# A hybrid decoder layer on one Trainium2 core: nine places for the early adaLN weights, and every second weight piece of the middle split by way of PSUM

## The chip, the cores and the metric

One core of one Trainium2 chip runs the whole program. The metric is the device time of one execution in microseconds (us). The engines are PE (TensorE matmul) and its weight loads PEld, DVE (VectorE), ACT (ScalarE), POOL (GpSimd) and SP (SyncE); each takes its instructions in program order, and SP and ACT also issue transfers.

## What is computed

One decoder layer in fp32 for 512 prompt tokens and 8 sample tokens, held as 520 columns. The part that matters here:

```python
sh1, sc1, g1, sh2, sc2, g2 = adaln(c, w_ada, b_ada)       # silu(c) @ w_ada + b_ada, in six parts
h = rmsnorm(x, pre1_g) * (1 + sc1) + sh1
... = jnp.split(h @ w_in, SPLIT_OFFSETS, axis=-1)         # then DeltaNet heads and sparse attention
mix = jnp.concatenate([o_a, o_b], axis=-1) @ w_out
x = x + g1 * rmsnorm(mix, post1_g)
h = rmsnorm(x, pre2_g) * (1 + sc2) + sh2
f = jnp.square(jax.nn.relu(h @ w_ff1)) @ w_ff2
x = x + g2 * rmsnorm(f, post2_g)
```

## The kernel before

**Three products for one.** Each fp32 product is made of three PE passes in a rounded format. A weight tile `wr` and an activation are each split into a high part (`wh`, `hh`) and the rest (`wl`, `hl`): ACT rounds (`wh = copy(wr)`, L327 or L431) and DVE subtracts (`wl = wr - wh`, L328). `mm3` then issues `wh*hh`, `wh*hl` and `wl*hh` (L446 to L448).

**The list of operations.** `run` writes one list of operations with the weights that each needs. `sub` hands out the next split piece; it also issues loads some items ahead (`load_to`) and splits some pieces ahead into a ring of six 512-column slots. Raw `wr` tiles have four places. A tile scheduler then sets each engine's order by what it expects to be ready. All loads of weights are issued by SP, in program order: a load that waits for a place holds every load behind it.

**The head.** The layer's inputs `x` (16 transfers), the constants and then the adaLN weights for the first norm (`wd`, 64 items of 512 KB, kind "ada") come in. `wd` tiles have four places (`L`, tag "d", `ND` = 4), and `LOOK` = 5 items are loaded ahead. The 16 blocks of the model dimension are taken in five parts, `PARTS`, of 2, 2, 4, 4 and 4 blocks. For each part `ada_part` multiplies the `wd` items (L590), sums the four column groups with a small matmul (L600), and `modulate` makes `hh` and `hl` of the part. Between two parts, `early` multiplies the finished part with eight weight columns while the `wd` of the next part go by. `norm` makes the row scale R of the first rmsnorm: a sum over partitions on PE (L310), a reciprocal root on DVE (L294 to L300), a transpose on PE (L275). It stands behind seven of the first part's eight `wd` items (`NORM` = 7).

**The middle.** `wout` multiplies with w_out (16 tiles). `mid` then makes the second norm's input for each half of the columns: `residual` (L1844 to L1861) scales `y`, adds x, squares and sums on DVE, ACT and POOL together; a second rmsnorm follows (L1890 to L1901), and the result is split into `h2h` and `h2l`. While it runs, PE is in `wout` or `ff1` on the other half. `xsums` then adds and splits the operands `T` of the later stage. Weights are split by `split1` here: ACT, then DVE with both inputs in SBUF.

**The units.** The later matmuls (`ff1_unit`, `ff2_unit`) use seven products for eight. Their weights go through `split_staged`: ACT rounds, ACT also copies `wr` into PSUM (`stg`, L436), and DVE subtracts with one input from PSUM (L437). POOL makes sums of weights (L374) meanwhile.

Of the kernel before, what the change touches and what calls it, by code (L numbers as in the profile page):

```python
# [9 lines left out]
F32 = mybir.dt.float32  # L10
# [35 lines left out]
NE = 8  # L46
PARTS = ((0, 2), (2, 4), (4, 8), (8, 12), (12, 16))
ADA0 = [[4 * k0 + 2 * (k1 - k0) * v for v in range(2)] for k0, k1 in PARTS]
NORM = 7
LOOK = 5  # L50
AD0 = 8
RY = 2
MY = 1
# [184 lines left out]
class Kern:  # L238
# [4 lines left out]

    def __init__(self, ctx, tc, I, O):
        self.ctx, self.tc, self.nc, self.I, self.O = ctx, tc, tc.nc, I, O
        self.jobs, self.more = [], None

    def open(self, name, side="left", **kw):
        st = ExitStack()
# [102 lines left out]
    def load_to(self, k):  # L352
        while self.iload <= min(k, len(self.items) - 1):
            ap, kind = self.items[self.iload]
            if kind == "more" and not self.more:
                return
            if kind == "ada":
                t = self.L("wd", [128, 1024])
            elif kind == "more":
                t = self.more()  # L360
            else:
                t = self.wp.tile([128, 1024], F32, name="wr", bufs=4)[:, :ap.shape[1]]
            self.nc.sync.dma_start(t, ap)
            self.raw[self.iload] = t
            self.iload += 1
# [10 lines left out]
    def sub(self):  # L376
# [4 lines left out]
            for key in [key for key in d if (key[0] if d is self.sums else key) < k]:  # L381
                del d[key]
        look = 7 if isinstance(now, str) else 4 if self.items[min(k + 4, len(self.items) - 1)][1] == "more" else 2
        self.load_to(k + (LOOK if self.items[min(k + LOOK, len(self.items) - 1)][1] == "ada" else look))
        while self.sumq and self.sumq[0][0] <= i + 2 + SL:
            _, ku, name = self.sumq.pop(0)
            self.wsum(ku, name)
        while self.icut < len(self.subs) and (self.icut <= i + 2 or self.ahead < 3):
# [7 lines left out]
            if not src:  # L396
                self.load_to(k)
                self.cut[self.icut] = self.raw[k]
            else:
                if src is True or src[0] == "A":  # L400
                    k += 0 if src is True else UNIT.index(src)
                    self.load_to(k)
                    wr = self.raw[k][:, o:o + n]
                else:
                    wr = self.sums[k, src][:, o:o + n]
                self.held[self.icut] = self.need(n)
                if n > 512 and self.slot % 2:
                    self.slot = (self.slot + 1) % RING
                a = 512 * self.slot
                self.slot = (self.slot + (n + 511) // 512) % RING  # L410
                wh, wl = self.wh[:, a:a + n], self.wl[:, a:a + n]
                if n > 512 and self.stage:
                    self.split_staged(wr, wh, wl)
                else:
                    self.split1(wr, wh, wl)
                self.cut[self.icut] = (wh, wl)
                self.ahead += 1
# [10 lines left out]
    def split_staged(self, x, hh, hl):  # L428

        nc = self.nc  # L430
        nc.scalar.copy(hh, x)  # L431
        n = x.shape[1]
        for o in range(0, n, self.stage[1]):
            s = slice(o, o + self.stage[1])
            p = self.stage[0].tile([128, self.stage[1]], F32, name="stg")
            nc.scalar.copy(p, x[:, s])  # L436
            nc.vector.tensor_tensor(hl[:, s], p, hh[:, s].bitcast(F32), op=OP.subtract)  # L437

# [92 lines left out]
    def head(self):  # L531
# [2 lines left out]
        hp, self.close_hp = self.open("hp", "right")  # L534
        self.hh = hp.tile([128, KT, NT], F32R, name="hh")
        self.hl = hp.tile([128, KT, NT], F32R, name="hl")
        self.kp, self.close_kp = self.open("kp")
        self.U, self.close_U = self.open("U")
        self.ada_tile = lambda: self.B("ada_t", [128, 16, 32])
        self.vacc = {}  # L540
        cr = self.B("cr", [128, 16, 9])
# [5 lines left out]
        nc.vector.tensor_scalar(cr, cr, 0.5, None, op0=OP.mult)  # L547
        nc.vector.scalar_tensor_tensor(self.cs[:, :, 0:9], th, 1.0, cr, op0=OP.add, op1=OP.mult)
        self.x = [self.B("x", [128, NT]) for _ in range(KT)]
        for kt in range(KT):  # L550
            nc.sync.dma_start(self.x[kt], I["x"][:, kt])
        nc.sync.dma_start(self.cst, I["cst"])
        self.xs = self.S("xs", [128, KT, NS])
        nc.scalar.dma_start(self.xs, I["xs"])
        ss = self.B("ss", [128, NT])
# [1 line left out]
        for kt in range(1, KT):  # L557
            sq = self.B("sq", [128, NT])
            nc.scalar.activation(sq, self.x[kt], AF.Square)
            nc.vector.tensor_tensor(ss, ss, sq, op=OP.add)  # L560
        self.mod[0], self.mod[1] = (self.kp.tile([128, 16, 9], F32, name=f"ada{v}") for v in range(2))
        self.aq, self.ssx = {}, ss

    def norm(self):
# [1148 lines left out]
            self.gate(h, accs, getattr(self, "mx", None))  # L1713

    def open_in(self):
        self.ptab = self.kp.tile([1, 256], I32, name="ptab")
        self.nc.scalar.dma_start(self.ptab, self.I["pt"])
        self.kn = self.S("kn", [128, 2])
# [5 lines left out]
    def open_mix(self):  # L1724
# [2 lines left out]
        self.flush()  # L1727
        nc.scalar.dma_start(self.O["convp"], self.cpo)
        nc.scalar.dma_start(self.O["convs"], self.stc)
        self.close_U()  # L1730
        self.close_kp()
        mx, self.close_mx = self.open("mx")
        self.mx = (mx.tile([128, KT, NT], F32R, name="mh"), mx.tile([128, KT, NT], F32R, name="ml"))
        self.U, self.close_U = self.open("U2")
# [22 lines left out]
    def open_out(self):  # L1757
# [6 lines left out]
        self.h2 = {0: self.parts(self.V1, "a", "h2")}  # L1764
        self.y = [[self.V1.tile([128, 4, HF], F32, name="y", tag="a") for _ in range(4)] for _ in range(2)]
        self.more = lambda: self.V1.tile([128, 1024], F32, name="wd2", tag="s")
        self.wo, self.close_wo = self.open("wo", "right")
        self.ada_tile = lambda: self.V1.tile([128, 16, 32], F32, name="ada_t", tag="s")
        self.gate_gain(2, 1, self.wo)
# [359 lines left out]
    def open_accs(self, shape, wide, bufs):  # L2129

        p, c1 = self.open("psu", space=PSUM)
        q, c2 = self.open("pst", bufs=bufs, space=PSUM)
        self.stage = q, wide
        self.acc = lambda n: p.tile(shape, F32, name=f"acc{n}")
        self.close_accs = lambda: (c2(), c1())

# [144 lines left out]
```

## Time and profile before

| | |
|---|---|
| median of three runs | 2828.99 us (2827.51 to 2833.29) |
| the profiled execution | 2828.82 us |
| its span, first to last instruction | 2827.1 us |
| PE busy | 2681.5 us, 95% of the span |
| DVE, ACT, POOL busy | 60%, 56%, 40% |
| mean granted TensorE clock | 0.979 of full speed |

The profile lists the busy time of each engine, groups of instructions by line, what each wait ended with, and any stretch of time by itself. PE's records have modelled ends, so a busy PE may still be slow: the count of its matmuls in a stretch tells more. [...] "Idle before <- X" names the instruction or transfer whose end came last.

### The profile page before, as it was taken

The page shows a single profiled execution, that of the slowest core. Times are in us where ns is not written, and L with a number is a line of the kernel's source. Part 1 is how long each engine was busy: PE and PEld are TensorE (multiplying, and loading weights), DVE is VectorE, ACT ScalarE, POOL GpSimd, SP SyncE. Part 2 cuts the span into 40 slices and gives each one's busy share as a digit, 9 for nine tenths or more (in the row PEclk, how much of TensorE's full clock was granted, in tenths as well). Part 3 has the DMA queues.
Part 4 walks back from the last instruction along what each step waited for, and adds up shares of the span by engine and source line. Part 5 has one row for each costly group of instructions (what it writes and reads, how often), then busy time and mean ns, then how long its engine had stood idle before and what let it go on. Part 6 is the DMA issues. An engine that isn't in the chain of part 4 may idle for free.

```text
span 2827.1 us, 56292 instructions
## 1 busy us (share of the span) xinstructions
PE 2681.5 (95%) x21584; PEld 2484.1 (88%) x21584; DVE 1693.7 (60%) x3338; ACT 1573.3 (56%) x2780; POOL 1127.3 (40%) x907
## 2 busy tenths in 40 slices
PE   6999999999999999999998999999998999999996
PEld 3589977788888877888887999999998999999996
DVE  4465493357585455642687555555556677776767
ACT  3134322234544443233566677777778888887763
POOL 0000011123103342221454665656567777777514
PEclk9999999999999999999998999999999999999998
DMA  7853466764444555577665434343433333342454
GB/s 262 288 172 74 122 193 209 217 193 140 158 155 155 167 157 178 184 244 254 232 220 158 157 117 146 117 146 118 145 132 128 133 137 129 142 144 102 138 173 157
DMA packets 195126, 466.15 MB, mean 165 GB/s; under 512 B 25609, under 2 KB 76170, under 8 KB 194858
## 3 DMA queue, kind: packets, MB, share of 16 engines
q1 hardware_dynamic: 165616, 421.83, 44.8%
q10 hardware_dynamic: 27194, 36.53, 4.3%
q0 software_dynamic: 2048, 4.21, 0.5%
q8 instruction: 170, 2.79, 0.4%
q14 instruction: 98, 0.80, 0.1%
HBM read 413.57 MB, written 48.91 MB: 164 GB/s over the span
## 4 chain that ended last, share of the span: by engine, by line
PE 64%; DVE 6%; DMA 3%; issue 2%; ACT 2%; POOL 1%; SPq 0%; another core or an unknown queue 0%; ACTq 0%; DVEq 0%; POOLq 0%
PE acc L446 19%; PE acc L448 19%; PE acc L447 19%; DMA wr<-in_win 2%; PE m L481 2%; DVE wl L328 1%; PE m L275 1%; PE m L1140 1%; ACT wh L327 1%; PE m L1117 1%; ACT y L1901 0%; DVE cu L1301 0%; DMA rx<-mixd 0%; PE m L1482 0%; PE m L1639 0%
## 5 line engine op out<-in xcount | busy, mean ns | idle before, releaser
L437 DVE TENSOR_TENSOR wl<-stg,wh 128x512 fp32r<-128x512 f32 (+1 forms) x584 | 490.0, 867 | 308.6 <-ACT wh L431 300.0
L446 PE MATMUL acc<-hh,wh 128*128 128x260 f32 (+1 forms) x1984 | 587.5, 298 | 14.3 <-ACT hh L622 5.7
L447 PE MATMUL acc<-hl,wh 128*128 128x260 f32 (+1 forms) x1984 | 568.1, 287 | 0.4 <-DVE hl L623 0.4
L448 PE MATMUL acc<-hh,wl 128*128 128x260 f32 (+1 forms) x1984 | 566.0, 287 | 1.6 <-DVE wl L328 1.6
L327 ACT CAST wh<-wr 128x512 fp32r<-128x512 f32 (+1 forms) x478 | 284.3, 611 | 462.9 <-DMA wr<-in_win 210.7
L328 DVE TENSOR_TENSOR wl<-wr,wh 128x512 fp32r<-128x512 f32 (+1 forms) x478 | 353.0, 753 | 312.8 <-ACT wh L327 309.1
L448 PE MATMUL acc<-xf,wl 128*128 128x260 f32 x1824 | 516.4, 283 | 4.6 <-DVE wl L328 4.6
L446 PE MATMUL acc<-xf,wh 128*128 128x260 f32 x1824 | 516.7, 283 | 2.5 <-ACT f L2162 1.1
L447 PE MATMUL acc<-xf,wh 128*128 128x260 f32 x1824 | 515.9, 283 | 0.0
L446 PEld LDWEIGHTS acc<-hh,wh 128*128 128x128 f32 (+1 forms) x1984 | 376.3, 190 | 88.6 <-issue 44.7
L447 PEld LDWEIGHTS acc<-hl,wh 128*128 128x128 f32 (+1 forms) x1984 | 377.3, 190 | 7.9 <-DVE hl L623 3.7
L448 PEld LDWEIGHTS acc<-hh,wl 128*128 128x128 f32 (+1 forms) x1984 | 376.4, 190 | 6.6 <-DVE wl L328 4.1
L448 PEld LDWEIGHTS acc<-xf,wl 128*128 128x128 f32 x1824 | 344.3, 189 | 5.0 <-DVE wl L328 4.9
L446 PEld LDWEIGHTS acc<-xf,wh 128*128 128x128 f32 x1824 | 344.3, 189 | 3.1 <-ACT f L2162 1.3
L447 PEld LDWEIGHTS acc<-xf,wh 128*128 128x128 f32 x1824 | 344.0, 189 | 0.0
L436 ACT COPY stg<-S 128x512 f32<-128x512 f32 (+1 forms) x334 | 240.7, 731 | 88.0 <-DVE wl L437 80.3
L448 PE MATMUL acc<-h2h,wl 128*128 128x260 f32 x928 | 267.6, 289 | 10.2 <-DVE wl L328 9.2
L446 PE MATMUL acc<-h2h,wh 128*128 128x260 f32 x928 | 267.2, 288 | 8.0 <-ACT wh L327 4.3
L447 PE MATMUL acc<-h2l,wh 128*128 128x260 f32 x928 | 267.7, 289 | 4.8 <-DVE h2l L328 4.8
L446 PE MATMUL acc<-T,wh 128*128 128x260 f32 x896 | 254.5, 284 | 4.7 <-DVE fr L2008 3.8
L448 PE MATMUL acc<-T,wl 128*128 128x260 f32 x896 | 254.4, 284 | 0.0
L447 PE MATMUL acc<-T,wh 128*128 128x260 f32 x896 | 254.0, 283 | 0.0
(543 smaller groups left out, 5798.6 us busy)
## 6 DMA issues: line engine op xcount, KB each, us to landing
wr<-in_wff SPq DMA_DIRECT2D x256, 512.0 KB
wd<-in_wada SPq DMA_DIRECT2D x106, 512.0 KB
wr<-in_win SPq DMA_DIRECT2D x106, 512.0 KB
wr<-in_wada SPq DMA_DIRECT2D x86, 512.0 KB
wr<-in_wout SPq DMA_DIRECT2D x48, 512.0 KB
st<-f SPq DMA_DIRECT2D x32, 520.0 KB
pg<-in_ckt SPq DMA_DIRECT2D x256, 64.0 KB
wr<-in_wff2l SPq DMA_DIRECT2D x32, 512.0 KB
```

The source lines that it names most:

```text
L275: self.nc.tensor.transpose(out, in_, self.ident[:n, :n])
L327: pin(self.nc.scalar.copy(hh, x))
L328: pin((eng or self.nc.vector).tensor_tensor(hl, x, hh.bitcast(F32), op=OP.subtract))
L436: nc.scalar.copy(p, x[:, s])
L437: nc.vector.tensor_tensor(hl[:, s], p, hh[:, s].bitcast(F32), op=OP.subtract)
L446: T.matmul(acc, wh[:, cs], xh, start=first, stop=False, skip_group_check=goes_on)
L447: T.matmul(acc, wh[:, cs], xl, start=False, stop=False, skip_group_check=goes_on)
L448: T.matmul(acc, wl[:, cs], xh, start=False, stop=last, skip_group_check=goes_on)
L481: self.nc.tensor.matmul(self.aacc[v][32 * g:32 * g + 32, :], self.cs[:, kt, :], w[:, j * 512:(j + 1) * 512], start=(kt == 0), stop=(kt == ...
L1117: nc.tensor.matmul(ps[:, :w], qs[h2][:, 128 * i:128 * (i + 1)], kb[:, :w], start=True, stop=True)
L1140: nc.tensor.matmul(po[:, 0:256], vt[:, kb_ + k], pts[:, 256 * k:256 * k + 256], start=(kb_ + k == 0), stop=(kb_ + k == i))
```

## The change

It changes the head and the middle.

- **Places.** A pool `eb` with five more `wd` places is open during the head; items whose number modulo 9 is under 5 go there, the rest to the four old places. While it is open, 12 items are loaded ahead in place of 5 (`EARLY_LOOK`). It closes in `open_in`, where the pool `kp` now opens, and two small tiles of `kp` move to another pool.
- **Order.** `NORM` goes from 7 to 2, and the load of the constants and of the first `wd` item is written ahead of `x`.
- **Split by way of PSUM.** In the middle (`wout` and the first 16 `ff1` operations) `stage` now stands for the PSUM tiles that small results use, and of the 512-column pieces every second one takes `split_staged`.

```diff
-NORM = 7
+NORM = 2
 LOOK = 5
+FIRST = 1
+EARLY_LOOK = 12
+EB = 5
...
-            if kind == "ada":
+            if kind == "ada" and self.eb and self.iload % 9 < EB:
+                t = self.eb.tile([128, 1024], F32, name="wd", bufs=EB)
+            elif kind == "ada":
                 t = self.L("wd", [128, 1024])
...
-        self.load_to(k + (LOOK if self.items[min(k + LOOK, len(self.items) - 1)][1] == "ada" else look))
+        look = EARLY_LOOK if self.eb else LOOK if self.items[min(k + LOOK, len(self.items) - 1)][1] == "ada" else look
+        self.load_to(k + look)
...
-                if n > 512 and self.stage:
+                if self.stage and (n > 512 or self.icut % 2):
                     self.split_staged(wr, wh, wl)
...
-            s = slice(o, o + self.stage[1])
-            p = self.stage[0].tile([128, self.stage[1]], F32, name="stg")
+            s = slice(o, min(n, o + self.stage[1]))
+            p = self.stage[0].tile([128, self.stage[1]], F32, name="stg", **self.stage[2])
...
-        self.kp, self.close_kp = self.open("kp")
         self.U, self.close_U = self.open("U")
+        self.eb, self.close_eb = self.open("eb")
...
+        nc.sync.dma_start(self.cst, I["cst"])
+        self.load_to(FIRST - 1)
         for kt in range(KT):
             nc.sync.dma_start(self.x[kt], I["x"][:, kt])
-        nc.sync.dma_start(self.cst, I["cst"])
+        self.mod[0], self.mod[1] = (hp.tile([128, 16, 9], F32, name=f"ada{v}") for v in range(2))
...
     def open_in(self):
+        self.close_eb()
+        self.eb = None
+        self.kp, self.close_kp = self.open("kp")
...
         self.more = lambda: self.V1.tile([128, 1024], F32, name="wd2", tag="s")
+        self.stage = self.psm, 512, {"tag": "m"}
```

The lines of the changed file stand 3 to 11 further on: L590 is L597 there, L275 L278, L310 L313, L600 L607, L363 L368, L328 L331, L437 L443, L1844 L1855, L1847 L1858, L1798 L1809.

On SP, the loads behind `x` in the head, before (`wd` and `wr` as above; PE_ and DVE_ are waits for a place or a result of that engine, DMAHW_ a wait for an earlier transfer):

```order
L363 DMA wd<-in_wada 128x1024 [waits DMAHW6_49]
L363 DMA wd<-in_wada 128x1024 [waits DMAHW7_49,PE_49]
L363 DMA wd<-in_wada 128x1024 [waits DMAHW4_49,DMAHW0_49,PE_49]
L363 DMA wd<-in_wada 128x1024 [waits DMAHW5_49,DMAHW1_49,PE_49]
L363 DMA wd<-in_wada 128x1024 [waits DMAHW6_49,DMAHW2_49,PE_49]
L363 DMA wr<-in_win 128x256 [waits DMAHW3_49]
```

The same loads after:

```order
L368 DMA wd<-in_wada 128x1024 [waits DMAHW2_49]
L368 DMA wd<-in_wada 128x1024 [waits DMAHW3_49]
L368 DMA wd<-in_wada 128x1024 [waits DMAHW4_49]
L368 DMA wd<-in_wada 128x1024 [waits DMAHW5_49]
L368 DMA wd<-in_wada 128x1024 [waits DMAHW6_49]
L368 DMA wr<-in_win 128x256 [waits DMAHW7_49]
```

The order is the same; the waits for PE are gone from the fifth to the eighth item. The first loads on SP (c, the constants, the first `wd`, then `x`) stand in the same order in both.

On PE, the start of the program before (four rows of L590 are one `wd` item of the first part; L310 and L275 are `norm`, `ss` its sum of squares, `rq_i` the reciprocal root, `aqs` the summed adaLN product):

```order
L590 MATMUL m<-wd,cs 32x256 x24
L310 MATMUL m<-ones,ss 128x1 x2
L310 MATMUL m<-ones,ss 4x1
L310 MATMUL m<-ones,ss 128x1 x2
L310 MATMUL m<-ones,ss 4x1
L590 MATMUL m<-wd,cs 32x256 x5
L275 MATMUL m<-cst,rq_i 128x128 x2
L275 MATMUL m<-cst,rq_i 128x4
L275 MATMUL m<-cst,rq_i 128x128 x2
L275 MATMUL m<-cst,rq_i 128x4
L590 MATMUL m<-wd,cs 32x256 x3
L600 MATMUL m<-cst,aqs 128x9 x4
```

The same after:

```order
L597 MATMUL m<-wd,cs 32x256 x16
L313 MATMUL m<-ones,ss 128x1 x2
L313 MATMUL m<-ones,ss 4x1
L313 MATMUL m<-ones,ss 128x1 x2
L313 MATMUL m<-ones,ss 4x1
L278 MATMUL m<-cst,rq_i 128x128 x2
L278 MATMUL m<-cst,rq_i 128x4
L278 MATMUL m<-cst,rq_i 128x128 x2
L278 MATMUL m<-cst,rq_i 128x4
L597 MATMUL m<-wd,cs 32x256 x16
L607 MATMUL m<-cst,aqs 128x9 x4
L597 MATMUL m<-wd,cs 32x256 x8
```

`norm` moved ahead of the last four items of the first part, and two items of the next part, not one, now stand ahead of the first `early`.

On DVE, the start of `residual` for the first half in the middle, before (`y` are its steps, `wl` the weight splits):

```order
L328 TENSOR_TENSOR wl<-wr,wh 128x512 x3
L1844 TENSOR_TENSOR y<-y,R 128x1040
L328 TENSOR_TENSOR wl<-wr,wh 128x512
L1798 TENSOR_TENSOR y<-acc,rg 128x8
L1847 TENSOR_TENSOR y<-y,rx 128x1040 x2
L1844 TENSOR_TENSOR y<-y,R 128x1040
L328 TENSOR_TENSOR wl<-wr,wh 128x512 x2
```

The same after:

```order
L331 TENSOR_TENSOR wl<-wr,wh 128x512
L1855 TENSOR_TENSOR y<-y,R 128x1040
L443 TENSOR_TENSOR wl<-stg,wh 128x512
L1809 TENSOR_TENSOR y<-acc,rg 128x8
L1858 TENSOR_TENSOR y<-y,rx 128x1040
L443 TENSOR_TENSOR wl<-stg,wh 128x512
L331 TENSOR_TENSOR wl<-wr,wh 128x512
L1858 TENSOR_TENSOR y<-y,rx 128x1040
L1855 TENSOR_TENSOR y<-y,R 128x1040
L443 TENSOR_TENSOR wl<-stg,wh 128x512
```

Among the steps of `residual`, pieces from PSUM (`stg`) now alternate with pieces from SBUF. Over the program 80 pieces of 512 columns, and the first two pieces of the units (as four of 512), change from SBUF to PSUM: 84 more subtractions with `stg` on DVE and 84 more `stg` copies on ACT. Between the head and the middle, and from the units on, the order of PE, DVE and ACT is the same.

## Rows read from the trace of the kernel before

**Rows 1.** Page, part 1: busy us, share of the span, instructions of each engine.
```profile
PE 2681.5 (95%) x21584; PEld 2484.1 (88%) x21584; DVE 1693.7 (60%) x3338; ACT 1573.3 (56%) x2780; POOL 1127.3 (40%) x907
```
**Rows 2.** Stretches: length; busy us and (instructions) by engine; clock; DMA share, GB/s.
```profile
63.00:92.00 29.00, 26.29 (x158) 16.05 (x160) 12.19 (x29) 3.91 (x9) 0.00 (x0) 0.94 0.80 277
99.00:132.00 33.00, 32.44 (x241) 25.32 (x238) 13.51 (x28) 5.27 (x9) 0.00 (x0) 0.97 0.76 264
...
1385.00:1425.00 40.00, 35.91 (x280) 34.79 (x279) 38.49 (x51) 20.66 (x38) 27.89 (x19) 0.96 0.62 215
1425.00:1445.00 20.00, 16.29 (x112) 15.19 (x111) 17.17 (x28) 17.67 (x33) 7.76 (x4) 0.83 0.37 129
1445.00:1480.00 35.00, 32.24 (x253) 31.62 (x252) 30.50 (x28) 18.07 (x34) 26.18 (x13) 0.95 0.76 242
1480.00:1520.00 40.00, 27.49 (x162) 24.93 (x162) 36.38 (x34) 25.89 (x47) 29.92 (x16) 0.75 0.28 91
1380.00:1580.00 200.00, 173.91 (x1289) 167.96 (x1288) 162.49 (x197) 121.69 (x212) 113.79 (x61) 0.90 0.56 183
1600.00:1800.00 200.00, 200.00 (x1669) 200.00 (x1669) 108.57 (x129) 150.69 (x180) 120.42 (x80) 1.00 0.39 130
```
**Rows 3.** Short stretches of the head, same columns.
```profile
20.00:22.00 2.00, 0.00 (x0) 0.00 (x0) 1.79 (x3) 1.66 (x3) 0.00 (x0) 1.00 1.03 416
...
48.00:52.00 4.00, 4.00 (x39) 2.97 (x38) 0.85 (x2) 1.86 (x6) 0.00 (x0) 1.00 0.53 160
...
68.00:72.00 4.00, 4.00 (x26) 2.43 (x24) 1.43 (x4) 0.41 (x1) 0.00 (x0) 1.00 0.19 21
```
**Rows 4.** Waits of SP's queue, 26 to 175 us: total us, times, longest.
```profile
SPq L363 <- PE m L590: 88.1, 38, 6.9
```
**Rows 5.** Waits of PE, 42 to 175 us, same columns.
```profile
PE m L590 <- DMA wd<-in_wada: 1.6, 2, 1.4
```
**Rows 6.** Timeline of the head on PE: start us, us, what, idle before.
```profile
28.44 2.18 PE L310 MATMUL m<-ones,ss 128*128 128x1 f32 x11
...
32.94 1.69 PE L275 MATMUL m<-cst,rq_i 128*128 128x128 f32 x6 [0.26 <-DVE rms_st L312]
...
34.56 1.07 PE L590 MATMUL m<-wd,cs 128*32 128x256 f32 x6
35.57 1.88 PE L600 MATMUL m<-cst,aqs 128*128 128x9 f32 x8
...
40.08 1.02 PE L446 MATMUL acc<-hh,wh 128*128 128x260 f32 x3 [1.62 <-ACT hh L622]
```
**Rows 7.** A transfer issued by ACT, timeline near the head's end.
```profile
168.31 0.34 ACTq L1721 DMA_DIRECT2D oh<-in_oh  x1
```
**Rows 8.** Weight subtractions by shape in 1220:1380, 1370:1580, 2150:2650: busy us, mean ns.
```profile
L328 DVE TENSOR_TENSOR wl<-wr,wh 128x512 fp32r<-128x512 f32 x66 | 45.7, 693 | 111.7 <-ACT wh L327 111.7
...
L328 DVE TENSOR_TENSOR wl<-wr,wh 128x512 fp32r<-128x512 f32 x96 | 93.1, 1001 | 18.9 <-ACT wh L327 18.9
...
L437 DVE TENSOR_TENSOR wl<-stg,wh 128x512 fp32r<-128x512 f32 x348 | 224.2, 686 | 95.1 <-ACT wh L431 90.3 <-ACT stg L436 4.7
```
**Rows 9.** Timelines of DVE and of POOL in the middle.
```profile
1391.79 2.92 DVE L328 TENSOR_TENSOR wl<-wr,wh 128x512 fp32r<-128x512 f32 x1
1428.43 2.93 DVE L328 TENSOR_TENSOR wl<-wr,wh 128x512 fp32r<-128x512 f32 x1
1436.85 0.16 DVE L314 TENSOR_SCALAR rms_st<-m 128x2 f32<-128x2 f32 x1 [2.45 <-PE m L310]
...
1388.10 6.06 POOL L1844 TENSOR_TENSOR y<-y,R 128x1040 f32<-128x1040 f32 x2 [3.27 <-ACT R L324]
1424.46 6.34 POOL L1890 TENSOR_TENSOR y<-y,R 128x1040 f32<-128x1040 f32 x2 [3.86 <-ACT R L324]
```
**Rows 10.** Waits of PE, 1180 to 1600 us.
```profile
PE acc L448 <- DVE wl L328: 13.0, 8, 3.2
```
**Rows 11.** The copy to PSUM, by shape, 2150:2650: busy us, mean ns.
```profile
L436 ACT COPY stg<-wr 128x512 f32<-128x512 f32 x149 | 87.4, 589 | 37.6 <-DVE wl L437 37.2
```

More of the change, by code (lines that the diff above doesn't have):

```diff
@@ L245, in __init__ @@
         self.ctx, self.tc, self.nc, self.I, self.O = ctx, tc, tc.nc, I, O
-        self.jobs, self.more = [], None
+        self.jobs, self.more, self.eb = [], None, None
     def open(self, name, side="left", **kw):
@@ L560, in head @@
             nc.vector.tensor_tensor(ss, ss, sq, op=OP.add)
-        self.mod[0], self.mod[1] = (self.kp.tile([128, 16, 9], F32, name=f"ada{v}") for v in range(2))
         self.aq, self.ssx = {}, ss
@@ L1729, in open_mix @@
         nc.scalar.dma_start(self.O["convs"], self.stc)
+        self.close_kp()
         self.close_U()
-        self.close_kp()
         mx, self.close_mx = self.open("mx")
@@ L2132, in open_accs @@
         q, c2 = self.open("pst", bufs=bufs, space=PSUM)
-        self.stage = q, wide
+        self.stage = q, wide, {}
         self.acc = lambda n: p.tile(shape, F32, name=f"acc{n}")
```

## Prediction

> **What bounds the kernel now.** I began with the busy times of the page. PE is busy for 2681.5 us of 2827.1 and no other engine comes near it [rows 1], so a gain has to come from time in which PE waits or runs slowly. The second view is the table of stretches, and what to see in it is the number of matmuls. In 1600 to 1800 us, with nothing in PE's way, 1669 matmuls pass in 200 us, one every 0.120 us. From 1380 to 1580 there are 1289, which at that pace is 154.5 us of work: 45.5 us are lost, though PE reads as busy for 173.9 [rows 2]. Of them 6.5 are lost in 1385 to 1425, 6.6 in 1425 to 1445, 4.7 in 1445 to 1480 and 20.6 in 1480 to 1520, by the same count [rows 2]. That is the middle, the one great loss that the diff touches. In the head PE is idle for 2.7 us in 63 to 92 and 0.6 us in 99 to 132, and it had a mean clock of 0.94 in the one and 0.97 in the other [rows 2].
>
> The third view is the waits. In the head SP's queue waits 88.1 us, in 38 waits, for PE to give back a `wd` place [rows 4]. Meanwhile the DMA engines, which moved 416 GB/s while nothing stopped them, fall to 160 and to 21 GB/s [rows 3]. So loads stop and later arrive late, though PE's own named waits for `wd` are only 1.6 us [rows 5]. In the middle PE's named wait is for `wl`, 13.0 us in 8 waits [rows 10], so DVE is what comes last there.
>
> The fourth view tells why DVE is late. A subtraction of 512 columns takes 693 ns in 1220 to 1380, and 1001 ns on average in 1370 to 1580 [rows 8]. The long ones take 2.92 and 2.93 us, and at those moments POOL is in a large operation of `residual` or of the second norm [rows 9]. The same subtraction with one input from PSUM takes 686 ns on average over 348 pieces of the units [rows 8], where POOL is busy 120 of 200 us [rows 2]. I read this as a stall that two SBUF inputs meet beside POOL, and that a PSUM input escapes.
>
> **The change part by part. Places and look-ahead.** Five more places let SP issue the fifth to the eighth item and those behind them without waiting for PE, so the 88.1 us of SP's waits shrink. No time is won by that itself: it is won where data came late. The bounds are 1.6 us, the waits named for `wd` [rows 5], and all the idle time of the two stretches, 3.3 us; I take 2.7, since the rest of the idle time waits for `wr` or a split behind the same blocked queue. To that comes the clock. A mean of 0.94 over 29 us, between the levels 1 and 0.5, is 3.5 us at 1.2 GHz, of which half, 1.7 us, is lost; 0.97 over 33 us loses 1.0. Both stretches are ones in which PE stood idle as well, so half of this 2.7 us should go with the idle time: I take 1.4, with bounds of 0 and 2.7.
>
> **Norm.** `norm` moves from behind six `wd` items, as PE has them, to behind four. Its sum on PE starts at 28.44 and its last transposes end at 34.56 [rows 6]. Two items at 416 GB/s are 2 x 1.26 us [rows 3], so those now end near 32.0. Four items then follow at 1.01 us each (34.56 to 35.57 is one), and the sum over groups (L600), at 35.57 before, comes at 36.1: 0.5 us late. Against it, one more item stands ahead of the first `early`, in PE's wait of 1.62 us for `hh` [rows 6], and that is 1.0 us won. Net -0.5 us; the bounds are +0.5 (the moved item gains nothing) and -1.0. The cover of this edit is that wait for `hh`; without it the 0.5 us are lost. The first loads stand in the same order on SP as before, so writing the constants first costs and gains nothing.
>
> **Pool kp.** It opens at the head's end, so ACT issues three more small loads there. One such issue took 0.34 us [rows 7], together 1.0 us; they stand in front of ACT's splits of the next weights, which are some pieces ahead, so I take 0.4 and keep 0 and 1.0.
>
> The head: -2.7 - 1.4 - 0.5 + 0.4 = -4.2 us, taken as -4. Its ends are -6.5 (3.3 + 2.7 + 1.0 - 0.5) and +1.5 (nothing gained, 0.5 and 1.0 paid).
>
> **Split by way of PSUM.** In 1370 to 1580 there are 96 subtractions of 512 columns, each 308 ns longer than undisturbed: 29.6 us [rows 8]. With every second one at 686 ns, half of it, 14.8 us, is taken off DVE. In the worst stretch DVE is busy 36.4 of 40 us while PE loses 20.6 [rows 2], so most of this reaches PE: I take 12. The order adds something. In the second norm DVE waits 2.45 us for PE's sum [rows 9]; subtractions of `h2l` now stand ahead of that row and fill the wait: I take 2. Fewer gaps also bring back some clock: 1480 to 1520 ran at 0.75 [rows 2], which is half of 40 us at 1.2 GHz and so 10 us lost; I take 2 of them. Against this, PE meets the second norm's sum earlier in its own work: +1, an estimate from the same 2.45 us.
>
> The new work is 84 copies into PSUM of 589 ns [rows 11], 49.5 us of ACT, which is busy 121.7 of 200 us in 1380 to 1580 [rows 2]. What hides it is the 78 us in which ACT has nothing; behind a copy in ACT's queue stand the next `wh` and the steps of `residual`. I put it at nothing, and the second rival has its price. PSUM places of small results are shared with the copies; DVE empties each in 0.69 us.
>
> The middle: -12 - 2 - 2 + 1 = -15 us. Its ends: -25, all 14.8 and the 10 us of clock; and -4, where another chain than DVE's binds (below).
>
> [...]
>
> **Sum.** 2828.8 - 4 - 15 = 2809.8 us, against the profiled execution's 2828.8 (its span and 1.7 us around it). The median is 2829.0, so nothing is to be converted.
>
> **The rivals. First, another chain binds the middle.** PE there waits for `h2h` of the other half in the end, and this comes by the reciprocal root, POOL's steps of 6.06 and 6.34 us for two [rows 9], and ACT. If that chain sets the end, freed DVE time only shortens DVE's own steps in it. I put that at 4 us: the 2.45 us wait and two stalls of the 2.2 us that 2.92 has over 0.69 [rows 9], 6.9 us, of which about half is in the chain. With the head's -4 the time is 2828.8 - 8 = 2821. For it: the 20.6 us are lost in the 40 us just behind the second norm. Against it: DVE is 36.4 of 40 us busy then, and PE names `wl` [rows 10].
>
> **Second, slower: ACT becomes the bound.** A piece of 512 columns feeds 12 matmuls. In 1425 to 1520 there are 112 + 253 + 162 = 527 matmuls, 44 pieces, 22 of them staged: 13.0 us more on ACT. If each copy holds back the next `wh` and nothing there is won, the time is 13.0, less 2.5 gained in 1385 to 1425 and 5 in the head: 2834, and up to 2841 with the head at +1.5. It decides if ACT is full wherever PE waits. For it: 1425 to 1445 holds 9.3 pieces, so 4.7 copies or 2.7 us, and ACT, busy 17.67 of 20, has 2.3 left [rows 2]. Against it: over all 95 us it is busy 61.6 (17.67 + 18.07 + 25.89) and has 33 left for 13 [rows 2].
>
> **Third, the head gives nothing.** The four `wr` places still hold SP's queue, and loads wait behind them as they did behind `wd`. Then the time is 2828.8 - 15 = 2814. For it: PE's named waits for `wd` are only 1.6 us [rows 5]. Against it: SP names PE's L590, not a `wr` place, in 88.1 us [rows 4].
>
> **How the numbers follow.** A measurement of this kernel can tell about 0.2%, 5.7 us, from no change, so faster means under 2823.3. The forecast of 2810 has 0.60, the first rival 0.18, the third 0.11, the second 0.06, and 0.05 is left for no change, where what DVE gains ACT takes. The forecast's own ends are 2828.8 - 6.5 - 25 = 2797 and, with both parts at their poor ends, 2828.8 + 1.5 - 4 = 2826; this takes in the first and third rival, and with the second outside it the range is 2797 to 2826. Faster is 0.84: the forecast, the third rival and most of the first, less 0.05 for poor ends. Same is 0.10 and slower 0.06.
>
> **What the profile after would show.** The head: SP's waits for the `wd` matmuls fall well under 88 us, idle time in 63 to 132 under 1 us. If these waits move to `wr` and PE's idle time stays, the third rival holds. The middle: `wl` from PSUM takes about 0.69 us beside POOL; the mean of all subtractions in 1370 to 1580 falls from 1001 to about 850 ns; 1380 to 1580 holds some 120 more matmuls. If the subtractions shorten and the matmuls do not rise, the first rival holds; if PE then waits for `wh` or `stg` and ACT has no idle time in 1425 to 1520, the second. The forecast is wrong if pieces from PSUM too take over 2 us beside POOL, since then nothing is freed and 49.5 us of ACT are paid.

## The result and the profile after

The changed kernel takes 2805.71 us (median of four runs, 2801.07 to 2812.09) where the kernel before takes 2830.08 (2827.51 to 2833.29). The ratio on record, from all runs, is 0.9931, with a 95% interval of 0.991 to 0.9952: 19.5 us faster, between 14 and 25. The two medians lie 24.4 us apart, inside that interval. The forecast was 19 us, so the total came out right. Its two parts did not: the head won about 11 us in place of 4, the middle some 7 in place of 15.

The first view is the table of stretches, for the whole head and for 260 us of the middle, beginning at the same matmul of the program in both kernels. The columns are those of [rows 2]. The kernel before:

```profile
0.00:230.00 230.00, 197.51 (x1392) 146.32 (x1393) 119.53 (x316) 76.84 (x185) 7.60 (x25) 0.98 0.66 225
1380.00:1640.00 260.00, 233.91 (x1789) 227.96 (x1788) 195.43 (x236) 166.30 (x265) 150.02 (x85) 0.92 0.53 174
```

The changed kernel:

```profile
0.00:230.00 230.00, 200.34 (x1489) 155.79 (x1490) 125.56 (x327) 80.79 (x195) 8.67 (x25) 0.97 0.66 230
1359.80:1619.80 260.00, 234.63 (x1849) 230.22 (x1848) 183.34 (x243) 194.46 (x322) 149.27 (x88) 0.95 0.54 180
```

Read the matmul counts, not PE's busy time. In the first 230 us 97 more matmuls pass, and at 0.120 us each ([rows 2], 1600 to 1800 us) that is 11.6 us. In the middle 60 more pass, 7.2 us, though PE's busy time grew by 0.7 us only. DVE's busy time there fell by 12.1 us, and ACT's rose by 28.2.

The two profiled executions differ by 27.8 us, 9 more than these two parts. The rest lies between the head and the middle, where the order of instructions is the same. From the 1380th matmul of the program to the 10220th the kernel before took 1150.1 us and the changed one 1141.8; over all traces of this study that stretch took between 1141.8 and 1158.3 us with the same instructions. No cause is read from it, and single executions of whole programs are not compared below.

The waits of SP's queue from 20 to 175 us, in the changed kernel:

```profile
SPq L368 <- PE m L597: 59.9, 22, 9.0
SPq L368 <- DVE wl L331: 33.7, 16, 8.8
```

Before, in the same 20 to 175 us, the waits for PE's `wd` matmuls were 90.0 us, and those for a `wr` place that DVE has to give back were these:

```profile
SPq L363 <- DVE wl L328: 7.4, 8, 3.7
```

So the waits for PE fell to 59.9 us, not to near nothing, and waits for `wr` took their place, as the third rival had it: together they are 97.4 us before and 93.6 after. The two stretches of the head that the prediction priced [rows 2], in the changed kernel:

```profile
63.00:92.00 29.00, 26.38 (x157) 15.37 (x157) 14.67 (x32) 7.48 (x14) 0.82 (x2) 0.88 0.91 329
99.00:132.00 33.00, 31.63 (x222) 22.95 (x221) 16.31 (x32) 7.93 (x14) 0.82 (x2) 0.90 0.92 330
```

The loads flow more freely, 329 and 330 GB/s where it was 277 and 264. But PE is idle for 2.6 and 1.4 us, together 4.0 where it was 3.3, and the clock is lower, 0.88 and 0.90 where it was 0.94 and 0.97. The prediction's sign for the head, under 1 us of idle time from 63 to 132, did not come. Both signs of the third rival came, but not its result: the head won 11 us all the same.

DVE's operations by shape from 1350 to 1560 us, busy us and mean ns, in the changed kernel:

```profile
L331 DVE TENSOR_TENSOR wl<-wr,wh 128x512 fp32r<-128x512 f32 x49 | 46.2, 943 | 12.2 <-ACT wh L330 9.3 <-PE acc L454 2.8
L443 DVE TENSOR_TENSOR wl<-stg,wh 128x512 fp32r<-128x512 f32 x52 | 35.2, 684 | 18.8 <-ACT stg L442 13.7 <-ACT wh L437 4.7
L1858 DVE TENSOR_TENSOR y<-y,rx 128x1040 f32<-128x1040 f32 x8 | 16.6, 2072 | 0.0
L331 DVE TENSOR_TENSOR T<-y,T 128x1040 fp32r<-128x1040 f32 x8 | 13.8, 1719 | 1.3 <-ACT T L330 1.3
L331 DVE TENSOR_TENSOR h2l<-y,h2h 128x1040 fp32r<-128x1040 f32 x8 | 13.5, 1692 | 6.6 <-ACT h2h L330 6.6
...
L1901 DVE TENSOR_TENSOR y<-y,R 128x1040 f32<-128x1040 f32 x4 | 7.9, 1974 | 1.3 <-ACT R L327 1.3
L1855 DVE TENSOR_TENSOR y<-y,R 128x1040 f32<-128x1040 f32 x4 | 6.6, 1650 | 2.0 <-ACT R L327 2.0
```

The large operations of the same stretch before:

```profile
L1847 DVE TENSOR_TENSOR y<-y,rx 128x1040 f32<-128x1040 f32 x8 | 13.5, 1702 | 0.0
L328 DVE TENSOR_TENSOR h2l<-y,h2h 128x1040 fp32r<-128x1040 f32 x8 | 12.9, 1609 | 2.6 <-ACT h2h L327 2.6
L328 DVE TENSOR_TENSOR T<-y,T 128x1040 fp32r<-128x1040 f32 x8 | 12.1, 1511 | 0.1
L1890 DVE TENSOR_TENSOR y<-y,R 128x1040 f32<-128x1040 f32 x4 | 9.9, 2482 | 0.0
L1844 DVE TENSOR_TENSOR y<-y,R 128x1040 f32<-128x1040 f32 x4 | 7.7, 1928 | 0.0
```

Within one stretch the pieces with one input from PSUM take 684 ns and those with both inputs in SBUF 943: the stall is there, and PSUM escapes it. Single records say the same. From 1350 to 1600 us of the kernel before, 62 SBUF pieces have no tensor_tensor of POOL beside them and take 0.68 to 0.70 us; 39 have one beside them for over half of their time and take 1.46 us on average, up to 2.93. In the changed kernel, 1330 to 1580 us, 26 PSUM pieces have one beside them like this, and each takes 0.68 or 0.69. 52 pieces at 317 ns less than the 1001 of [rows 8] are 16.5 us. Of the large operations the steps with `rx`, T and `h2l` are 5.3 us longer together than before, the row scales with R 3.1 us shorter; all of them have two inputs in SBUF and can still meet POOL (a T takes 1.23 to 1.24 us alone and up to 3.47 beside it).

PE's waits from 1360 to 1640 us, in the changed kernel:

```profile
PE acc L454 <- DVE wl L443: 10.0, 6, 3.9
PE acc L452 <- ACT wh L437: 5.5, 4, 2.1
PE acc L453 <- DVE h2l L331: 3.5, 3, 2.3
PE acc L452 <- ACT h2h L330: 2.5, 1, 2.5
```

`wl`, 13.0 us in [rows 10], is still first, now of pieces that themselves take 0.68 us. They stand in DVE's queue behind something else, or wait for ACT: of DVE's idle time ahead of the PSUM pieces 13.7 us ended with the copy `stg`.

### The profile page after: what moved, and what is told of

Its sections match the earlier page's. It is cut to its first block, busy times and chain, and to the rows that moved or that the text cites. A ratio compares the mean times of both kernels' runs of the same rounds, so it can differ in the third digit from the quotient of the medians.

```text
span 2799.3 us, 56366 instructions
## 1 busy us (share of the span) xinstructions
PE 2661.9 (95%) x21584; PEld 2475.3 (88%) x21584; DVE 1676.3 (60%) x3340; ACT 1611.8 (58%) x2864; POOL 1122.1 (40%) x907
## 5 line engine op out<-in xcount | busy, mean ns | idle before, releaser
L443 DVE TENSOR_TENSOR wl<-stg,wh 128x512 fp32r<-128x512 f32 (+1 forms) x668 | 547.4, 844 | 386.9 <-ACT wh L437 363.6
L452 PE MATMUL acc<-hh,wh 128*128 128x260 f32 (+1 forms) x1984 | 586.4, 297 | 12.8 <-ACT hh L629 5.2
L452 PE MATMUL acc<-xf,wh 128*128 128x260 f32 x1824 | 517.5, 284 | 2.0 <-DVE f L2175 0.9
L452 PEld LDWEIGHTS acc<-hh,wh 128*128 128x128 f32 (+1 forms) x1984 | 375.4, 190 | 84.3 <-issue 48.0
L330 ACT CAST wh<-wr 128x512 fp32r<-128x512 f32 (+1 forms) x397 | 235.0, 608 | 344.7 <-DMA wr<-in_win 189.7
L331 DVE TENSOR_TENSOR wl<-wr,wh 128x512 fp32r<-128x512 f32 (+1 forms) x397 | 280.8, 717 | 238.2 <-ACT wh L330 231.5
L452 PEld LDWEIGHTS acc<-xf,wh 128*128 128x128 f32 x1824 | 344.9, 189 | 2.7 <-ACT wh L330 1.1
L442 ACT COPY stg<-wr 128x512 f32<-128x512 f32 (+1 forms) x332 | 229.8, 697 | 114.0 <-DVE wl L443 86.0
L452 PE MATMUL acc<-h2h,wh 128*128 128x260 f32 x928 | 265.9, 287 | 8.0 <-ACT wh L437 5.5
L437 ACT CAST wh<-wr 128x1024 fp32r<-128x1024 f32 (+1 forms) x248 | 225.1, 908 | 83.1 <-PE acc L453 76.4
L452 PE MATMUL acc<-T,wh 128*128 128x260 f32 x896 | 254.6, 284 | 5.3 <-DVE fr L2019 3.9
```

The source lines that it names most:

```text
L330: pin(self.nc.scalar.copy(hh, x))
L331: pin((eng or self.nc.vector).tensor_tensor(hl, x, hh.bitcast(F32), op=OP.subtract))
L452: T.matmul(acc, wh[:, cs], xh, start=first, stop=False, skip_group_check=goes_on)
```

## Experiments

Matmuls are counted in the order of the program, all 21584 of which are in every trace. "Head" is by how much the 1380th stands earlier than in the kernel before, where it is at 228.5 us. "Middle" is the number of matmuls in 260 us that begin 1 to 2 us behind the 10220th; one more is 0.12 us. These two are from one trace each, the ratio from all runs against the kernel before on the same chip.

| kernel | ratio (95% interval) | head, us | middle |
|---|---|---|---|
| before | 1 | 0 | 1789 |
| changed | 0.9931 (0.991 to 0.9952) | 12.0 | 1849 |
| head_only | 0.9957 (0.9938 to 0.9976) | 12.7 | 1776 |
| stage_only | 0.9969 (0.9956 to 0.9982) | 2.8 | 1852 |
| stage_all | 0.9929 (0.991 to 0.9949) | 12.6 | 1844 |
| copy_twice | 0.9982 (0.9969 to 0.9995) | 12.1 | 1761 |
| look5 | 0.9964 (0.995 to 0.9979) | 12.6 | 1774 |
| norm7 | 0.9963 (0.9946 to 0.998) | 6.0 | 1781 |
| small_early | 0.9951 (0.992 to 0.9981) | 10.5 | 1797 |
| xsums_late | 0.9933 (0.991 to 0.9956) | 12.8 | 1803 |
| xsums_3 | 0.9933 (0.991 to 0.9956) | 10.5 | 1835 |
| xsums_dve | 0.9923 (0.9897 to 0.995) | 11.9 | 1877 |
| scale_dve | 0.9909 (0.988 to 0.9938) | 11.8 | 1860 |
| both_dve | 0.9906 (0.989 to 0.9921) | 10.4 | 1890 |

The spread of one column is seen in it: stage_only has the head of the kernel before and shows 2.8 us, and the kernels with the changed head show 10.4 to 12.8. The changed head is thus worth 8 to 13 us. In the middle the five kernels with the splits of before hold 1774 to 1797 matmuls, 2.8 us apart. Single places repeat better: from the 11000th to the 11080th matmul these five lose 20.7 to 21.0 us against the pace of one matmul in 0.12 us.

**The two halves.** head_only takes the split by way of PSUM out of the changed kernel:

```diff
-        self.stage = self.psm, 512, {"tag": "m"}
```

> The head of the changed kernel (places, look-ahead, order, pool kp) with the middle's splits as before. Theory from the two traces (head won 12 us, middle 7, the rest differs from run to run): the matmuls behind the head stand 11 to 13 us earlier than before, the middle loses 46 us as before, and the time is about 12 us under the kernel before, 2818. Rival, the sizes of the prediction (head 4, middle 15): 2826.

stage_only puts this line, and the choice of every second piece, into the kernel before.

> The kernel before with every second middle piece split by way of PSUM, and its head as before. Theory: the middle loses some 39 us in place of 46, the time is about 7 us under the kernel before, 2823. Rival, the sizes of the prediction: 15 us, 2815. If the stretch from 300 to 1100 us, where the two traces also differ by 8 us though the order there is the same, moves with this part of the change, the time would be about 2815 as well, but the matmuls of the middle would show 7 us.

By the ratios head_only is 12.1 us faster (0.43%; the medians lie 6.9 us apart) and stage_only 8.7 us (0.31%; medians 5.4). Together the ratios give 20.8, so the parts add up to the 19.5 of the whole within the intervals. Both came out by the theory, and the prediction's sizes of 4 and 15 fall: by the intervals, and more firmly by the matmuls. 63 more in the middle of stage_only make the split worth 7.6 us there, and the head of head_only ends 12.7 us earlier.

**What the head's gain is made of.** norm7 has `norm` at its old place, the rest as head_only.

```diff
-NORM = 2
+NORM = 7
```

> head_only with norm at its old place behind seven items. The prediction priced this move at 0.5 us. Theory from the trace of the changed kernel, where PE's matmuls pass at half pace until 46 us before and until 38 us after: the move lets PE run without a gap earlier, and is worth 3 us or more by the 140th matmul, so here that matmul stands only 3 to 4 us earlier than before instead of 7. Rival (the prediction's size): 6.5 us earlier.

The 140th matmul stands 2.9 us earlier than before and the head's end 6.0, against 7.0 and 12.7 in head_only. The kernels with the early `norm` end their heads 10.4 to 12.8 us earlier, so by norm7's one trace the move is worth 4 to 7 us and is the largest part of the head. The ratios, 0.9963 and 0.9957, can't confirm it: their intervals are wider than that. The timeline of PE shows what differs. head_only (start us, us, operation, idle before):

```profile
28.34 1.69 PE L278 MATMUL m<-cst,rq_i 128*128 128x128 f32 x6 [2.30 <-DVE rms_st L315]
29.96 2.87 PE L597 MATMUL m<-wd,cs 128*32 128x256 f32 x32
32.76 1.19 PE L607 MATMUL m<-cst,aqs 128*128 128x9 f32 x8
...
36.75 0.62 PE L452 MATMUL acc<-hh,wh 128*128 128x260 f32 x3 [1.80 <-ACT hh L629]
...
57.04 0.63 PE L452 MATMUL acc<-hh,wh 128*128 128x260 f32 x3 [0.66 <-ACT hh L629]
```

norm7:

```profile
31.13 1.69 PE L278 MATMUL m<-cst,rq_i 128*128 128x128 f32 x6 [0.54 <-DVE rms_st L315]
...
33.76 1.88 PE L607 MATMUL m<-cst,aqs 128*128 128x9 f32 x8
...
38.26 1.02 PE L452 MATMUL acc<-hh,wh 128*128 128x260 f32 x3 [1.62 <-ACT hh L629]
...
60.64 0.68 PE L452 MATMUL acc<-hh,wh 128*128 128x260 f32 x3 [1.27 <-ACT hh L629]
```

With `norm` early, PE waits 2.30 us for DVE's root. In that time the four items that follow come in, and they pass in 2.80 us, 0.70 each. L607 begins at 32.76 where norm7 has it at 33.76, and the first `early` 1.5 us earlier. The next matmuls run at full pace at once (three rows of L452 in 0.62 us against 1.02). In norm7 the pace goes from one matmul in 0.22 us to one in 0.12 only at 41.7 us, which makes another 2.5 us.

This lead at the start is not `norm`'s alone. In xsums_dve, whose engines run the head in the same order as head_only's, the first `early` begins at 38.29 us and full pace, one matmul in 0.12 us, comes only near 45, so the 140th matmul stands 2.5 us earlier than before, no more than in norm7. Of the eleven kernels with the early `norm` six reach full pace at 32 to 33 us, two at 41 and three (look5, xsums_dve, small_early) at 44 to 46.

What stands in every trace comes later. Before the second `early`, one more item fills the wait for `hh`: 0.66 us of it is left in all eleven, where the three kernels with the late `norm` (before, stage_only, norm7) have 1.27 or 1.28. The stretches of norm7 just behind it show what that cost:

```profile
63.00:64.00 1.00, 1.00 (x7) 1.00 (x6) 0.28 (x1) 0.00 (x0) 0.00 (x0) 0.50 0.76 282
64.00:65.00 1.00, 1.00 (x4) 0.44 (x4) 0.99 (x4) 0.21 (x1) 0.00 (x0) 0.50 0.96 345
```

The granted clock is 0.50 for some 3.5 us, in which a matmul of 260 columns passes in 0.22 us and not in 0.12; it fell there in all three kernels with the late `norm` and in none of the eleven others. From the 200th to the 300th matmul the three take 16.4 to 17.0 us and the eleven 14.0: 2.4 to 3.0 us of the 4 to 7 are shown in this way.

look5 keeps the nine places and goes back to 5 items of look-ahead while they are there.

```diff
-EARLY_LOOK = 12
+EARLY_LOOK = 5
```

> The head of the changed kernel without the split by way of PSUM (as head_only), and with 5 items loaded ahead in place of 12; nine places and the order stay. Theory: the head's start (the first wd items and norm) gains its 6 to 7 us as in head_only, and the 5 us that head_only gained from the 140th to the 540th matmul, by loads that don't wait, are mostly gone: 2 us or less of them stay. Time 2820 where the kernel before has 2828 (or 7 us under it). Rival: the places alone do it, and the head ends 12 us earlier as in head_only.

The rival held. The 140th matmul stands only 3.2 us earlier than before, but by the 740th look5 has caught up, and the head ends 12.6 us earlier. head_only loses 2.5 us of its lead in one place: from 82 to 90 us its clock fell to 0.64 and 0.51, behind the same wait of 1.4 us for `hh` at which look5's stayed at 1.00. The late start is no effect of the shorter look-ahead either: xsums_dve, with 12 items, takes the same course. No run has the old places with the new order, so what the places give by themselves is known by subtraction alone.

small_early issues three small loads of the pool `kp` at the program's start again, by giving them places in another pool.

```diff
-        self.stc = kp.tile([128, 24, 8, 3], F32, name="stc")
+        self.stc = self.early_p.tile([128, 24, 8, 3], F32, name="stc")
```

(and likewise `cw` and `gng`)

> head_only, but three of the small loads that came with the late pool kp (cw, stc, gng) are issued at the program's start as before, from another pool. Theory: these loads, in small pieces, hold back the x and wd behind them; the second wd item is multiplied at 22.4 us as before and not at 20.3, and the head ends 2 us later than in head_only. Rival: the move of these loads costs ACT 0.4 us at the head's end and gains nothing at the start (the prediction's size); then the head ends 0.4 us earlier than in head_only.

The second `wd` item is multiplied at 21.8 us, against 20.1 to 20.5 in the eleven other kernels where these loads come late, so 1.2 to 1.6 us are due to these loads. At the head's end the difference is 2.2 us, but two kernels with the whole changed head end there too, so no more than the 1.2 to 1.6 is settled. What ACT pays for these loads at the head's end was not measured by itself. The kernel before shows the place, SP's and ACT's issues at its start:

```profile
3.21 12.81 SPq L551 DMA_DIRECT2D x<-in_x  x16
...
5.17 0.34 ACTq L1248 DMA_DIRECT2D cw<-in_convw  x1
6.92 0.34 ACTq L1251 DMA_DIRECT2D stc<-in_stc  x1
7.30 0.44 ACTq L1258 DMA_DIRECT2D gng<-in_gng  x1
```

The stretch of 8 to 12 us, before:

```profile
8.00:12.00 4.00, 0.00 (x0) 0.00 (x0) 0.70 (x1) 1.22 (x3) 0.47 (x1) 1.00 0.89 273
```

and after:

```profile
8.00:12.00 4.00, 0.00 (x1) 0.00 (x0) 2.38 (x4) 2.72 (x5) 0.00 (x0) 1.00 0.99 337
```

273 GB/s with the small loads on their way, 337 without; small_early, with three of them, has 272. The 16 issues of `x` took SP 12.81 us, and 10.89 in the changed kernel.

**Why the middle gave half.** stage_all splits every piece of the middle by way of PSUM.

```diff
-                if self.stage and (n > 512 or self.icut % 2):
+                if self.stage and True:
```

> The changed kernel with every middle piece split by way of PSUM, not every second. If DVE still binds where PE waits: the subtractions of the middle all take about 0.69 us, 12 us more are freed on DVE, and as the first half turned 15 us into 7, the time falls by about 5 more, 2801. If ACT binds by now: 48 more copies of 0.59 us put 28 us on ACT in the middle's 200 us, PE waits for wh and stg, and the time rises by up to 13 us, 2819. If the chain of the second norm binds: no difference, 2806.

copy_twice makes ACT's copy into PSUM twice in the middle.

```diff
             nc.scalar.copy(p, x[:, s])
+            if self.stage[2]:
+                nc.scalar.copy(p, x[:, s])
```

> The changed kernel, but in the middle ACT makes each copy into PSUM twice, 80 more copies of 0.59 us, 47 us more on ACT. If the copies are hidden in ACT's idle time, as the prediction had it: less than 3 us, up to 2809. If ACT already comes last in the middle: the 22 copies of the 95 us where PE waits are paid, 13 us, 2819.

stage_all is the changed kernel's equal: 1844 matmuls against 1849. All its `wl` take 685 ns, DVE is busy for 16.7 us less, and PE gets nothing of it; DVE's idle time that ends with `stg` rises from 13.7 to 24.1 us. copy_twice loses 88 matmuls, 10.6 us, and 0.5% of the time. So ACT's idle time covers the copies no longer. PE's waits in copy_twice, 1360 to 1600 us (its lines stand 2 further on):

```profile
PE acc L456 <- DVE wl L445: 15.3, 9, 3.5
PE acc L454 <- ACT wh L437: 12.2, 5, 3.4
```

The waits for `wh` rose from 5.5 to 12.2 us, and `wl` waits for a copy that comes late. How much the first copies already cost cannot be read from this, only that with every second piece the two engines are about level.

The place where the changed kernel loses most is the second half's `h2h` (DVE, and POOL beside it):

```profile
1480.45 2.85 DVE L331 TENSOR_TENSOR h2l<-y,h2h 128x1040 fp32r<-128x1040 f32 x1 [0.79 <-ACT h2h L330]
1483.22 0.68 DVE L443 TENSOR_TENSOR wl<-stg,wh 128x512 fp32r<-128x512 f32 x1
1483.82 2.84 DVE L331 TENSOR_TENSOR T<-y,T 128x1040 fp32r<-128x1040 f32 x1
1486.59 2.87 DVE L331 TENSOR_TENSOR wl<-wr,wh 128x512 fp32r<-128x512 f32 x1
...
1482.15 3.41 POOL L1953 TENSOR_TENSOR y<-y 128x1040 f32<-128x1040 f32 x1
1485.52 3.38 POOL L1959 TENSOR_TENSOR y<-y 128x1040 f32<-128x1040 f32 x1
```

A piece of 0.68 us stands behind an `h2l` of 2.85 and ahead of a `T` of 2.84, and POOL makes the sums T all the while. Four kernels act on this. xsums_late and xsums_3 begin the sums later:

```diff
-        ops.append(([], lambda: (self.flush(), self.spawn(self.xsums()))))
+        ops.append(([], lambda: (self.flush(), self.spawn(self.xsums(), 7))))
```

> The changed kernel with the sums T of the middle (subtractions on DVE and POOL with two SBUF inputs) begun seven steps later. In the changed kernel PE loses 19 us from the 11000th to the 11080th matmul, where DVE makes T and h2l of 2 to 3 us each beside POOL, between the subtractions that PE waits for. Theory: with T out of the way 6 to 9 us of this go, and the time falls to about 2798. Rival, the chain to h2h alone binds there: less than 2 us, 2805. Second rival: T comes late for the stage behind, and PE waits there for as much as it won.

(xsums_3 has 4 for 7)

> As xsums_late, with the sums begun four steps later in place of seven. By xsums_late's trace PE won 5 us behind the 11020th matmul and lost 7 more than that behind the 11360th, where T came late. With four steps T is done three steps sooner: half of the gain stays (2 to 4 us) if the loss behind goes, so the time is about 2 us under the changed kernel's. If the loss behind stays over 3 us: no gain, or slower.

xsums_dve has POOL's part of the sums on DVE:

```diff
-        tt = self.nc.gpsimd.tensor_tensor
+        tt = self.nc.vector.tensor_tensor
```

> The changed kernel with the six subtractions that POOL makes for the sums T moved to DVE, in the same order. If what lengthens DVE's h2l and T (2.8 us each, from the 11000th to the 11080th matmul) is POOL's work beside them: they fall to 1.3 us, SBUF pieces there to 0.69, and though DVE has six operations of 1.25 us more, PE loses 2 to 5 us less there. If it isn't POOL: they stay at 2 to 3 us, DVE has 7.5 us more, and PE loses up to 7 us more.

scale_dve does the same with the second norm's row scale:

```diff
-            (nc.gpsimd if q % 2 else nc.vector).tensor_tensor(self.y[h][q], self.y[h][q], Rb, op=OP.mult)
+            nc.vector.tensor_tensor(self.y[h][q], self.y[h][q], Rb, op=OP.mult)
```

> The changed kernel with the second norm's row scale made on DVE for all four blocks, where POOL made two of them in 6.3 us. The places where PE waits for this chain (10600th to 10640th and 11000th matmul, 13 us in the kernel before and as much in the changed one) are what the first rival spoke of. If the chain binds there: DVE does the two in 2.6 us and PE waits 2 to 6 us less in the two places together. If DVE's own queue binds there: no gain, or up to 3 us lost.

xsums_late won 4.9 us of 19.0 from the 11000th to the 11080th matmul, less than the theory, and gave back 10.0 us more than the changed kernel from the 11360th to the 11460th: there the units begin, and T is late. That is the second rival; begun four steps later it is the same on a smaller scale, 5.1 us won and 4.6 more given back. xsums_dve holds 28 more matmuls than the changed kernel, 3.4 us. Its DVE operations, 1350 to 1560 us:

```profile
L331 DVE TENSOR_TENSOR wl<-wr,wh 128x512 fp32r<-128x512 f32 x53 | 45.6, 860 | 15.0 <-ACT wh L330 14.8
...
L331 DVE TENSOR_TENSOR h2l<-y,h2h 128x1040 fp32r<-128x1040 f32 x8 | 11.0, 1374 | 3.6 <-ACT h2h L330 3.4
L331 DVE TENSOR_TENSOR T<-y,T 128x1040 fp32r<-128x1040 f32 x8 | 9.9, 1236 | 0.3 <-ACT T L330 0.3
```

With POOL out of the way T takes 1236 ns, not 1719, and `h2l` 1374, not 1692. From the 11000th to the 11080th matmul PE lost 5.2 us less, and 1.6 more where the units begin. With the single records of the changed kernel, where a T alone takes 1.24 us and one beside POOL 2.84 or 3.47, this is the most direct evidence that POOL's work beside them is the cause of the stalls. scale_dve won 3.4 us at the 11000th matmul, where PE waits for `h2h` (5.4 to 2.0 us), and 0.9 from the 10600th to the 10660th was lost: 11 more matmuls, 1.3 us. DVE has more to do there and PE waits less, so the chain to `h2h` does bind at the 11000th, and not DVE's queue.

both_dve joins the two moves.

> The changed kernel with both moves to DVE: the six subtractions of POOL for the sums T, and the second norm's row scale of all four blocks. Alone they cut what PE loses in the middle from 38.8 us to 35.4 and to 37.4. If they act at different places, as the traces say (T behind the 11040th and 11360th matmul, the scale at the 11000th): 33 to 35 us, the time about 5 us under the changed kernel's, a ratio to the kernel before of 0.991 to 0.992. If DVE is full by now: no better than 35.4 us, and the ratio 0.993.

It holds 1890 matmuls, 41 or 4.9 us more than the changed kernel. Its time is 2798.32 us (median of six, 2793.27 to 2804.45), its ratio 0.9906 (0.989 to 0.9921), 26.6 us under the kernel before. Its row of the middle:

```profile
1362.90:1622.90 260.00, 237.51 (x1890) 233.11 (x1889) 179.98 (x256) 198.19 (x326) 122.22 (x81) 0.96 0.54 180
```

POOL is busy for 27 us less than in the changed kernel, and DVE, which took over its work, for 3 us less as well. The two moves add up: from the 11000th to the 11080th matmul they win 5.2 and 3.2 us alone and 8.5 together, of which 3.5 are lost again where the units begin. The intervals of both_dve and the changed kernel overlap; that it is the faster rests on the middle's matmuls, and is only made likely by the times.

## Why the prediction was right, and where it was not

**Places and look-ahead: the size not refuted, the mechanism not seen.** Priced at 2.7 + 1.4 = 4.1 us. norm7, with places, look-ahead and late small loads, ends its head 6.0 us earlier than the kernel before; less 1.2 to 1.6 for the small loads some 4.6 are left, and as the head of before has a spread of 2.8, anything from about 2 to 5 fits. The two terms are not seen in it. Over the same matmuls, the 140th to the 1380th, PE is idle for 8.5 us in the kernel before and 6.6 in norm7, but for 7.1 in stage_only too, which has the old places; and from the 300th to the 740th the mean clock is 0.90 in norm7 where it was 0.95. The 1.6 us of waits for `wd` [rows 5] were a poor base as well: stage_only shows 0.2. The look-ahead itself gave nothing that lasts (look5). The clock terms take half of the time at 0.50, there called 1.2 GHz, as lost. No trace gives GHz, only the share and the pace: in the kernel before a matmul of 260 columns passes in 0.218 us where the clock is 0.50, about 1.2 columns in a nanosecond, and in 0.120 where it is 1.00, so 45% is lost there.

**Norm: the step that failed in the head.** Priced at 0.5 us with bounds of +0.5 and -1.0; by norm7 it was 4 to 7. The sum took 1.01 us for an item from a stretch in which items came in at 1.26 us each and PE was slow, with one matmul of 260 columns in 0.22 us until 46 us. Items that were already there took 0.70 in head_only. It also let the moved item gain its own duration only. That the clock doesn't fall at 62 us, 2.4 to 3.0 us in every trace, was in no term: the clock term asked what fewer waits for data would bring, not what the item moved ahead of `early` would. The rest of the 4 to 7 us has no cause that the runs show: six of the eleven kernels win more at the start and lose part of it at 83 us, three do neither, two lie between, and their heads end within 2.4 us of one another. The far end of the forecast for the head, -6.5 us, holds a 0.5 that no term gives; by its own bounds it was -7.0, and 8 to 13 lies outside both.

**Pool kp: the wrong sign.** Priced as a cost of 0.4 us on ACT at the head's end. The prediction looked at where the loads went, not at where they had been: beside the loads of `x`, which they slowed. Moving them away gained 1.2 to 1.6 us at the start; the 0.4 itself stays unmeasured.

**Split by way of PSUM: the mechanism right, the size half.** 0.69 us beside POOL was forecast, 684 ns measured; 14.8 us freed on DVE, 16.5 measured. "Most of this reaches PE: I take 12" is the term that failed: with all other terms of the middle it came to 7 or 8. Of what was freed 5.3 us went to longer `rx`, T and `h2l` operations, of which shorter row scales gave 3.1 back. Where PE waits for the chain of the second norm (10600th to 10660th and 11000th matmul) it lost 12.8 us before and 13.5 after, so the 2 us for DVE's order were not won. That is the first rival's mechanism, at these two places and not in all of the middle; scale_dve shows that the second of them is the chain.

**ACT: "nothing" was too kind.** The idle time over 200 us did cover the copies so far that the change still won, but by copy_twice and stage_all nothing is left of it where PE waits. The mean share of busy time said 61%; the 17.67 of 20 us in 1425 to 1445 [rows 2], which the second rival cited, was the better guide. (That rival's own sum of 2834 holds 5 us for the head, where the forecast has 4, and 2.5 that no row gives.)

The total was right by luck: the head's error of -7 and the middle's of +7 or 8 cancelled.

## What to carry to other kernels

A load or step that is moved has a price at both ends: look at what it did to its neighbours where it was, as well as where it goes. When work is taken off a stalled engine, count how much of its remaining work can meet the same stall, and whether the engine that pays for the relief is level already where the bound engine waits: a second helping, or the payment made twice, shows that in one run. A step that waits for a long chain can be put where the data of the next steps are still on their way; here such a move came out as the largest part of the head, though one trace of each kernel leaves its size open.

## What was not expected of the hardware

**The clock column at the start.** One matmul of 260 columns is 0.42 us long in both of these kernels near 40 us, where it is 0.28 later. The stretch and the matmul, before:

```profile
42.00:44.00 2.00, 2.00 (x13) 1.97 (x10) 0.00 (x0) 0.00 (x0) 0.00 (x0) 1.00 0.43 103
...
42.63 0.42 PE L446 MATMUL acc<-hh,wh 128*128 128x260 f32 x1
```

and in both_dve:

```profile
38.00:40.00 2.00, 2.00 (x13) 0.96 (x13) 1.42 (x3) 0.47 (x2) 0.00 (x0) 0.50 0.50 111
...
39.87 0.42 PE L454 MATMUL acc<-hh,wl 128*128 128x260 f32 x1
```

The column says 1.00 in the one and 0.50 in the other, at the same pace of one matmul in 0.22 us. The 1.00 is no measurement: in the trace of before the first record of the granted clock begins at 46.26 us, just where the pace goes from one matmul in 0.22 us to one in 0.12, and a stretch without a record counts as 1.00 in the column. In both_dve the records begin at 23.91 us. So near the start of these kernels the pace of the matmuls tells more than that column.

**The same wait, two clocks.** Behind one and the same idle time of 1.4 us the clock fell to 0.5 for some 7 us in head_only and stayed at 1.00 in look5. It is not the look-ahead: it stayed at 1.00 in xsums_dve and small_early too, which load 12 items ahead. These three are the ones that reached full pace last, at 44 to 46 us; in the other eight the clock fell. Why was not tried.
